# A transformer block on one core: four DRAM additions move to other places on GpSimd, and the planner no longer reserves time for them

## The chip, the cores and the metric

The kernel runs on 1 core of one Trainium2 chip. The metric is the device time of one execution in microseconds; lower is better. The engines are TensorE (PE in the profile; PEld is its loading of weights), VectorE (DVE), ScalarE (ACT), GpSimd (POOL) and SyncE (SP), which only issues DMAs here. GpSimd can issue DMAs too; its queue is the only one that can add to what stands at the destination.

## What is computed

One decoder block in float32 on 512 tokens of width 1024: a norm, a projection into queries, keys and values, attention of two kinds, an output projection, a gated MLP with a short convolution, and a gated embedding at the end. Cut to what matters:

```python
proj = rmsnorm(x, attn_pre_g) @ w_in
o_nsa = nsa_attention(q_n, k_cmp, v_cmp, ksl, vsl, kwn, vwn, gates, slopes)  # 8 heads, 2 groups
o_swa = swa_attention(q_s, k_s, v_s, sinks, slopes)                          # 8 heads, 2 groups, window 128
mix = concat([o_nsa, o_swa]) @ w_o
x = x + rmsnorm(mix, attn_post_g)
a, u = split(rmsnorm(x, mlp_pre_g) @ w_gate_up)                              # 2816 wide each
y = (gelu(causal_dwconv(a)) * u) @ w_down
x = x + rmsnorm(y, mlp_post_g)
x = x + (p @ w_ple) * sigmoid(x @ w_ple_gate)
```

## The kernel before

**Precision and work.** Each float32 operand is split into a high and a low part, and a product is made of three TensorE products (high by high, low by high, high by low). So each weight tile costs a load by SP, a conversion on ACT (the high part) and a subtraction on DVE or GpSimd (the low part). For part of the MLP, products of blocks are combined by sums of weights, which saves products on TensorE. Some of these sums, of blocks of the down projection, are made ahead of time in DRAM.

**The DRAM sums.** With `DRAM_SUMS = 1`, one scratch tensor `downblocks` in DRAM gets four blocks of 384 KB by plain copies from SP (`down_copies`, in the order of blocks 2, 3, 0, 1). Then four accumulating DMAs on GpSimd's queue (`down_additions`, through `accumulate`) add to them: block 2 gets an input block, block 3 gets an input block, block 0 gets block 3, block 1 gets block 0. So the third addition reads what the second made, and the fourth what the third made. The sums are read much later, by the down projection from 459 us on.

**The attention.** `attention` walks through 16 units: 8 of the first kind (`nsa_scores`) and 8 local ones (`swa_scores`), each for a group `g` of heads and a tile `qt` of 128 queries, in the order qt = 3, 0, 2, 1. Of a local unit, TensorE makes the scores (`swa_pss`), DVE takes row maxima, ACT the exponentials, DVE the reciprocal sums, GpSimd scales the four heads' rows (`scale_rows`, four TENSOR_SCALAR on `swa_u`), TensorE transposes them (`swa_pst`), ACT and DVE split them, and TensorE multiplies with the values (`swa_pso`). Between these products, TensorE is fed "fillers", among them the first part of the output projection: `out_proj_first` is called for output tiles 0 to 3 (four blocks of the mix each) and then for tiles 4 to 7 (six blocks each). Its inner function `w(c)` loads the weights of output tile `c`, with the low part on GpSimd (`fill_wh<-fill_wr` on POOL).

**What sets the order.** From the start of the kernel to the end of the output projection, the instructions are not issued at once but recorded as nodes (`Recorder`). `play` then plans an order: it gives each node a cost (`cost`, times `MARGIN` except on TensorE, plus `more`), simulates the five engines in six passes with due times from the pass before, keeps the best order and issues the nodes in it, each held in program order. A node's `then` is a list of further calls that are made right behind it; the planner does not see them. A node's `more` is extra planned time that stands for them.

**Where the additions are.** Each of the first calls of `w(c)` takes a copy and hangs it behind its weight load on SP. For c = 1, 2, 3 and 6 (`ADDS_AT`) it also hangs the next addition behind its subtraction on GpSimd and gives that node `more = ADD_US`, 1.35 us.

**Behind the attention.** `out_proj` records the rest of the output projection, loads of the embedding weights and tiles (`pletiles`), the sums of squares of the result (`outproj_s`), and the first MLP weights (`upw`); then it calls `rec.play`. `norm_add` follows: TensorE sums the squares over the partitions (`r_pst<-ones,outproj_s`), GpSimd takes the inverse root (`r2c`), and the first MLP products wait for the rows that are scaled by it.

Of the kernel before, what the change touches and what calls it, by code (L numbers as in the profile page):

```python
# [20 lines left out]
KC = D // P  # L21
# [59 lines left out]
MARGIN = 1.08  # L81
# [21 lines left out]
ETAGS = ["mm", "mm"]  # L103
D_AT = 1
T_DUE = (15, 20, 30, 34, 38, 42)
ADD_US = 1.35
ADDS_AT = (1, 2, 3, 6)
DRAM_SUMS = 1


# [73 lines left out]
class Node:  # L184
    ins = None

    def __init__(self, n, engine, name, a, k):
        self.n, self.engine, self.name, self.a, self.k = n, engine, name, a, k
        self.deps, self.after, self.wait = set(), [], 0
        self.then, self.more = [], 0.0  # L190
        views = [x for x in a if isinstance(x, View)]
        named = [(m, x) for m, x in k.items() if isinstance(x, View)]
        first = [k["out"]] if "out" in k else [x for x in a[:1] if isinstance(x, View)]
        self.writes = first + [x for m, x in named if m == "accum_out"]
        self.reads = [x for x in views if not any(x is w for w in self.writes)] + [x for m, x in named if m not in ("out", "accum_out")]
        self.tiles = list({id(x.tile): x.tile for x in self.writes + self.reads}.values())
        self.end = None
# [37 lines left out]
class Recorder:  # L235
# [71 lines left out]
    def link(self):  # L307

        for x in self.nodes:
            for d in x.deps:  # L310
                d.after.append(x)
        for x in self.nodes:
            x.cost = self.cost(x) * (1 if x.engine == "PE" else MARGIN) + x.more
            x.port = x.engine == "POOL" or x.engine == "DVE" and x.name in SHARED and not any(v.tile.psum for v in x.reads)
            x.key = x.n if x.engine != "SP" else min([y.n for y in x.after] or [x.n])

# [124 lines left out]
class Block:  # L441
# [564 lines left out]
    def swa_scores(self, u):  # L1006
        self.phase = "swa"
        nc = self.nc
        g, qt = u["g"], u["qt"]
        kh, kl = self.ks  # L1010
        n = P if qt == 0 else 2 * P
        k0 = 0 if qt == 0 else (qt - 1) * P
        b0 = P if qt == 0 else 0

        p = self.u([P, P_WIDTH], F32, "p")[:, : 4 * (2 * P + 1)].rearrange("p (r n) -> p r n", r=4)
        ns = self.nsink[:, 4 * g : 4 * g + 4]
        nc.gpsimd.tensor_copy(p[:, :, n], ns)
        nm = self.tiny([P, 4], "nm")
        for r in range(4):
            if r % 2 == 0:  # L1020
                ps = self.ps("s")
            o = ps[:, r % 2 * 256 : r % 2 * 256 + 256]
            self.score(ps, o, self.q[4 + 2 * g + r // 2][:, r % 2, qt * P : (qt + 1) * P],
                       kh[:, g, k0 : k0 + 256], kl[:, g, k0 : k0 + 256])
            nc.vector.tensor_tensor_reduce(p[:, r, :n], o[:, :n], self.dist_w[:, b0:], op0=ALU.add, op1=ALU.min,
                                           scale=SLOPES[4 * g + r], scalar=ns[:, r : r + 1], accum_out=nm[:, r : r + 1])
            yield 100 if r < 3 else 4 * n + 380
        sm = self.tiny([P, 4], "sm")
        for r in range(4):
            nc.scalar.activation(p[:, r, : n + 1], p[:, r, : n + 1], AF.Exp, bias=nm[:, r : r + 1], scale=-1.0,  # L1030
                                 accum_out=sm[:, r : r + 1])
        rc = self.tiny([P, 4], "rc")
        nc.vector.reciprocal(rc, sm)
        for r in range(4):
            self.scale_rows(p[:, r, :n], rc[:, r : r + 1])
        yield 400
        u["blocks"] = [
            ([p[:, r, b * P : (b + 1) * P] for r in range(4)], P,
             self.vs[k0 // P + b][:, 4 + g].rearrange("p a d -> p (a d)"))
            for b in range(n // P)  # L1040
        ]
# [105 lines left out]
    def attention(self):  # L1147
# [48 lines left out]
        units += [dict(kind="s", g=g, qt=qt) for g in range(2) for qt in (3, 0, 2, 1)]  # L1196
        self.x1 = [None] * 4
        self.raws = {}
        copies, adds = self.down_copies(), self.down_additions()
        self.down_work = ((next(copies, None), next(adds) if i in ADDS_AT else None) for i in range(KC))  # L1200

        def fetch(key, src, tag):
            t = self.u([P, D], F32, tag)
# [56 lines left out]
    def out_proj_first(self, cs, n):  # L1260

        def w(c):
            at = len(self.rec.nodes)
            r = self.weight(self.io["wo"][c][:, : n * P], n * P, lo="pool")
            copy, add = next(self.down_work, (None, None))
            for x in self.rec.nodes[at:]:
                if copy and x.engine == "SP":
                    x.then.append(copy)
                if add and x.engine == "POOL":
                    x.then.append(add)  # L1270
                    x.more = ADD_US
            return r

        wts = [w(cs[0])]
        for i, c in enumerate(cs):
            if i + 1 < len(cs):
                wts.append(w(cs[i + 1]))
            ps = self.ps("mm")
            yield from self.mixmm(ps, wts[i], range(n))
            self.nc.scalar.activation(self.mo[c // 2][:, c % 2, :], ps, AF.Copy)  # L1280

    def out_proj(self):
        self.phase = "outproj"
        nc, io = self.nc, self.io
        acc = self.s([P, T])
        NS = 3
        run = lambda gen: [None for _ in gen]
        first = []
        for c in range(KC):
            if c < NS:  # L1290
                if c == 0:

                    first = [(self.ps(t), self.weight(io["wo"][i][:, 4 * P :], 4 * P, tag=w))
                             for i, (t, w) in enumerate((("mm", "tt"), ("s", "wh"), ("mm", "wh")))]
                    self.pinned = self.steps[-1]
                    for ps, wt in first:
                        run(self.mixmm(ps, wt, range(4, 6), 0, False))
                    self.pinned = None
                ps, wt = first[c]
                run(self.mixmm(ps, wt, range(6, 8), 2, True))  # L1300
            else:
                if c < SIX:
                    k = 4
                    wt = self.weight(io["wo"][c][:, k * P :], (KC - k) * P)
                else:
                    k = 6
                    if c == SIX:

                        n = KC - SIX
                        last = self.weight(io["wo"][SIX:, :, k * P :].rearrange("c p n -> p c n"), n * 2 * P)  # L1310
                    wt = [w[:, (c - SIX) * 2 * P : (c - SIX + 1) * 2 * P] for w in last]
                ps = self.ps("smsms"[c - NS] .replace("m", "mm"))
                run(self.mixmm(ps, wt, range(k, KC)))
            m = self.mo[c // 2][:, c % 2, :]
            nc.vector.tensor_add(m, m, ps)
            self.square_acc(acc, m, c == 0, True)
            if c == 2:
                ple = self.ple_load()
                self.phase = "outproj"
            if c == 4:  # L1320
                for j in range(4):
                    if j < 2:
                        x1 = self.raws[f"x{j}"].rearrange("p (c n) -> p c n", c=2)
                    else:
                        x1 = self.u([P, 2, T], F32, "p")
                        self.load_late(x1, io["xT"][:, 2 * j : 2 * j + 2, :])
                    self.x1[j] = x1
            if c == KC - 1:
                self.upw = [self.weight(self.raws[f"gu{i}"], early=True, keep=True) for i in range(2)]
                self.upw += [self.weight(io["gu"][i], tag=("tt", "u")[i - 2], keep=True) for i in range(2, NB)]  # L1330
        live = [(t, 0.0) for t in (*ple[0], *ple[1][0])] + [(acc, 3.2), *((t, 2.5) for t in ple[1][1])]
        live += [(t, 4.0) for t in (*self.mo, *self.x1, *ple[2])] + [(t, 7.0) for w in self.upw for t in w]
        self.rec.play(live, BEGIN, self.hold)
        self.h2, self.f2 = [], []
        self.acc3 = self.norm_add(acc, "r2", C_GPOST, self.mo, self.x1, C_GMLP, self.h2, ple, 0)

# [802 lines left out]
    def run(self):  # L2139
        self.consts()  # L2140
        self.attention()
        self.tc.cur_priority = LATE
        self.out_proj()
        self.mlp_up()
        self.mlp_down()
        self.ple_gate()
# [62 lines left out]
```

## Time and profile before

| | |
|---|---|
| Time, median of 3 runs | 625.67 us (625.45 to 626.41) |
| Profiled execution | 626.01 us, span 624.3 us |
| PE busy | 618.3 us (99%), 4037 products |
| DVE busy | 510.6 us (82%) |
| ACT busy | 399.3 us (64%) |
| POOL busy | 156.1 us (25%), 239 instructions |
| DMA | 95.79 MB, mean 153 GB/s |
| GpSimd's DMA queue (q0) | 4880 packets, 10.49 MB |

The stages stand in the profile as follows: the load and first projections until about 70 us, the attention until about 212 us, the rest of the output projection and the norm until about 241 us, the MLP's first half until about 475 us, its second half until about 595 us, and the gated embedding to the end.

How to read it: a timeline row gives the start in us, the time that the merged instructions took, the engine, the line, the operation, "written tile <- read tiles", the shape, the count, and in brackets the idle time before it and who ended it. Lines L216 and L435 are the helpers that issue all instructions, so one goes by tiles. Matmuls overlap, and their durations are modelled; differences between starts are the safer measure on PE. The issue of a DMA on GpSimd stands as DMA_DIRECT2D on POOL.

### The profile page before, as it was taken

How to read it: one execution, taken by the hardware profiler on the slowest of the kernel's cores; microseconds unless marked ns; L12 is line 12 of the kernel's file. 1: busy time of each engine (PE TensorE's matmuls, PEld its weight loads, DVE VectorE, ACT ScalarE, POOL GpSimd, SP SyncE). 2: the span in 40 equal slices, each digit the busy share in tenths (PEclk: the TensorE clock that was granted, in tenths of full speed). 3: DMA queues.
4: the chain of work that ended last, by engine and by line, in shares of the span. 5: the costliest groups of instructions: out<-in, count | busy, mean ns of one | idle time of the engine just before them, and what ended most of it. 6: DMA issues, size and time to landing. Idle time of an engine off the chain costs nothing.

```text
span 624.3 us, 11286 instructions
## 1 busy us (share of the span) xinstructions
PE 618.3 (99%) x4037; PEld 560.3 (90%) x4037; DVE 510.6 (82%) x1038; ACT 399.3 (64%) x776; POOL 156.1 (25%) x239
## 2 busy tenths in 40 slices
PE   9999999999999999999999999999999999999997
PEld 8988888888888887888999999999998899999986
DVE  6697569978866498799999999999999876947973
ACT  7546579889899577565677767777753443434251
POOL 2011397787788100121010101101000001201000
PEclk9999999999999999999999999999999999999999
DMA  8427923404422658285467777786443433378032
GB/s 295 163 94 208 240 83 93 111 22 125 117 77 69 218 237 336 91 242 158 119 147 209 184 176 178 191 213 163 99 135 117 136 93 110 95 286 300 6 120 83
DMA packets 45576, 95.79 MB, mean 153 GB/s; under 512 B 4560, under 2 KB 14160, under 8 KB 45264
## 3 DMA queue, kind: packets, MB, share of 16 engines
q1 hardware_dynamic: 40496, 84.57, 41.2%
q0 software_dynamic: 4880, 10.49, 10.0%
q8 instruction: 32, 0.52, 0.4%
q14 instruction: 24, 0.20, 0.1%
q10 hardware_dynamic: 144, 0.00, 0.0%
HBM read 81.42 MB, written 9.44 MB: 146 GB/s over the span
## 4 chain that ended last, share of the span: by engine, by line
PE 98%; DVE 1%; ACT 0%; issue 0%; ACTq 0%
PE mlpup_psmm L216 23%; PE fill_psmm L435 10%; PE mlpup_pss L216 8%; PE mlpdown_pst L216 6%; PE mlpup_pst L216 5%; PE mlpdown_pss L216 4%; PE mlpdown_psmm L216 4%; PE nsa_pss L435 3%; PE nsa_pso L435 3%; PE nsa_pst L435 3%; PE norm_pss L216 3%; PE projq_psmm L435 3%; PE vnatural_pss L435 2%; PE mlpup_pso L216 2%; PE projk_psmm L435 2%; PE compress_psmm L435 2%
## 5 line engine op out<-in xcount | busy, mean ns | idle before, releaser
L216 PE MATMUL mlpup_psmm<-r_u,mlpup_wh 128*128 128x256 f32 (+1 forms) x612 | 75.2, 276 | 0.0
L216 PEld LDWEIGHTS mlpup_psmm<-r_u,mlpup_wh 128*128 128x128 f32 x612 | 72.2, 188 | 0.2
L216 PE MATMUL mlpup_psmm<-mlpup_u,mlpup_wh 128*128 128x256 f32 (+1 forms) x474 | 67.1, 292 | 0.0
L216 PEld LDWEIGHTS mlpup_psmm<-mlpup_u,mlpup_wh 128*128 128x128 f32 x474 | 61.1, 188 | 2.6
L216 POOL DMA_DIRECT2D mlpup_u<-in_gs_dram x17 | 20.7, 1220 | 147.8 <-DVE mlpup_s L216 54.8
L216 ACT ACTIVATE mlpup_wh<-mlpup_u 128x1024 fp32r<-128x1024 f32 (+1 forms) x38 | 39.4, 1038 | 14.4 <-PE mlpup_psmm L216 10.8
L216 ACT ACTIVATE mlpdown_wh<-mlpdown_wr 128x1024 fp32r<-128x1024 f32 (+1 forms) x24 | 23.5, 981 | 34.6 <-DMA mlpdown_wr<-in_down_dram 9.2
L216 DVE TENSOR_TENSOR mlpup_wh<-mlpup_u,mlpup_wh 128x1024 fp32r<-128x1024 f32 (+1 forms) x38 | 45.1, 1190 | 0.3 <-ACT mlpup_wh L216 0.3
L435 PE MATMUL fill_psmm<-loadx_u,fill_wh 128*128 128x512 f32 x144 | 44.9, 400 | 0.0
L216 PE MATMUL mlpdown_pst<-mlpup_u,mlpdown_wh 128*128 128x512 f32 (+1 forms) x228 | 44.5, 337 | 0.0
L216 PEld LDWEIGHTS mlpdown_pst<-mlpup_u,mlpdown_wh 128*128 128x128 f32 x228 | 36.6, 188 | 4.8
L435 POOL TENSOR_SCALAR nsa_u<-nsa_u,nsa_nrc,vnatural_u 128x512 f32<-128x512 f32 (+3 forms) x64 | 38.4, 614 | 8.1 <-DVE nsa_nrc L435 6.6
L216 POOL TENSOR_TENSOR mlpdown_s<-mlpdown_s,mlpdown_s 128x512 f32<-128x512 f32 x6 | 10.1, 1692 | 120.5 <-ACT mlpdown_s L216 120.4
L216 DVE TENSOR_TENSOR mlpdown_wh<-mlpdown_wr,mlpdown_wh 128x1024 fp32r<-128x1024 f32 (+1 forms) x24 | 26.9, 1122 | 15.5 <-ACT mlpdown_wh L216 11.8
L435 ACT ACTIVATE nsa_u<-nsa_u,nsa_nnm 128x512 f32<-128x512 f32 (+3 forms) x64 | 35.4, 556 | 2.0 <-DVE nsa_nnm L435 1.7
L216 PE MATMUL mlpdown_pss<-mlpup_u,mlpdown_wh 128*128 128x256 f32 x246 | 34.9, 276 | 0.0
L216 DVE TENSOR_TENSOR mlpup_wh<-mlpup_wr,mlpup_wh 128x1024 fp32r<-128x1024 f32 (+1 forms) x23 | 27.9, 1211 | 5.9 <-ACT mlpup_wh L216 5.9
L216 PEld LDWEIGHTS mlpdown_pss<-mlpup_u,mlpdown_wh 128*128 128x128 f32 x246 | 31.5, 188 | 0.5
L216 ACT ACTIVATE mlpup_u<-mlpup_u 128x512 fp32r<-128x512 f32 (+1 forms) x36 | 21.5, 624 | 16.3 <-DVE mlpup_u L216 16.2
L216 PE MATMUL mlpdown_psmm<-mlpup_u,mlpdown_wh 128*128 128x256 f32 (+1 forms) x180 | 31.1, 317 | 0.0
L435 DVE CUSTOM_DVE_ANT_0 nsa_u<-nsa_pss,vnatural_u 128x128 f32<-128x128 f32 (+4 forms) x64 | 27.3, 445 | 3.3 <-PE nsa_pss L435 1.7
L435 POOL TENSOR_TENSOR fill_wh<-fill_wr,fill_wh 128x1024 fp32r<-128x1024 f32 (+2 forms) x13 | 24.9, 1918 | 17.5 <-DMA compress_u<-projk_u 9.3
(346 smaller groups left out, 1655.4 us busy)
## 6 DMA issues: line engine op xcount, KB each, us to landing
mlpup_u<-in_gs_dram SPq DMA_DIRECT2D x34, 512.0 KB, 5.5
mlpup_u<-in_gs_dram POOLq DMA_DIRECT2D x17, 512.0 KB, 6.0
mlpup_wr<-in_gs_dram SPq DMA_DIRECT2D x17, 256.0 KB, 2.8
fill_wr<-in_win_dram SPq DMA_DIRECT2D x6, 512.0 KB, 4.1
fill_u<-fill_u SPq DMA_DIRECT2D x20, 128.0 KB, 2.3
mlpdown_wr<-in_down_dram SPq DMA_DIRECT2D x5, 512.0 KB, 4.7
compress_u<-projk_u SPq DMA_DIRECT2D x16, 128.0 KB, 3.5
kept_e<-pletiles_u SPq DMA_DIRECT2D x4, 512.0 KB, 5.2
```

What stands on the lines that cost most here:

```text
L216: return f(*map(real, a), **{m: real(x) for m, x in k.items()})
L435: hold(x.call(*map(real, x.a), **{m: real(v) for m, v in x.k.items()}))
```

## The change

The planner's extra cost is removed: the constants `ADD_US` and `ADDS_AT`, the field `more`, and its part in the node's cost. The four additions hang in new places: the first still behind the subtraction of output tile 1's weights; the second and third behind the last scaling of rows of the local units (g = 0, qt = 0) and (g = 1, qt = 0); the fourth is issued right behind `rec.play`, so behind everything that was recorded. The copies stay behind the weight loads of output tiles 0 to 3. Nothing else differs.

```diff
             for d in x.deps:
                 d.after.append(x)
         for x in self.nodes:
-            x.cost = self.cost(x) * (1 if x.engine == "PE" else MARGIN) + x.more
+            x.cost = self.cost(x) * (1 if x.engine == "PE" else MARGIN)
...
         nc.vector.reciprocal(rc, sm)
         for r in range(4):
             self.scale_rows(p[:, r, :n], rc[:, r : r + 1])
+        if qt == 0:
+            self.rec.nodes[-1].then.append(self.adds[1 + g])
         yield 400
...
-        copies, adds = self.down_copies(), self.down_additions()
-        self.down_work = ((next(copies, None), next(adds) if i in ADDS_AT else None) for i in range(KC))
+        self.copies, self.adds = list(self.down_copies()), list(self.down_additions())
...
             r = self.weight(self.io["wo"][c][:, : n * P], n * P, lo="pool")
-            copy, add = next(self.down_work, (None, None))
             for x in self.rec.nodes[at:]:
-                if copy and x.engine == "SP":
-                    x.then.append(copy)
-                if add and x.engine == "POOL":
-                    x.then.append(add)
-                    x.more = ADD_US
+                if x.engine == "SP":
+                    x.then += self.copies[c : c + 1]
+                elif x.engine == "POOL" and c == 1:
+                    x.then.append(self.adds[0])
             return r
...
         self.rec.play(live, BEGIN, self.hold)
+        self.adds[3]()
         self.h2, self.f2 = [], []
```

More of the change, by code (lines that the diff above doesn't have):

```diff
@@ L105 @@
 T_DUE = (15, 20, 30, 34, 38, 42)
-ADD_US = 1.35
-ADDS_AT = (1, 2, 3, 6)
 DRAM_SUMS = 1
@@ L189, in __init__ @@
         self.deps, self.after, self.wait = set(), [], 0
-        self.then, self.more = [], 0.0
+        self.then = []
         views = [x for x in a if isinstance(x, View)]
```

## The prediction

> **What bounds the kernel now.** I read the page first, then the waits of PE, then PE's timeline in the one stretch where it loses time, then GpSimd's timeline (POOL) around the four additions, and last the stretch behind the attention where one of them is put.
>
> ```profile
> span 624.3 us, 11286 instructions
> PE 618.3 (99%) x4037; PEld 560.3 (90%) x4037; DVE 510.6 (82%) x1038; ACT 399.3 (64%) x776; POOL 156.1 (25%) x239
> ...
> PE 98%; DVE 1%; ACT 0%; issue 0%; ACTq 0%
> ```
> ```profile
> PE swa_pso L435 <- DVE swa_u L435: 0.2, 1, 0.2
> ```
>
> The chain that ended last is PE for 98% of the span, and behind the start PE waits visibly once, for 0.2 us. GpSimd is busy a quarter of the span. So nothing that is taken off GpSimd shows in the time unless PE was waiting for it, and anything that makes PE wait shows in full. A busy PE can hide lost time in a stretched matmul, so I compare starts with starts.
>
> ```profile
> 163.26 1.19 PE L435 MATMUL swa_pss<-projq_u,fill_u 128*128 128x256 f32 x8
> 164.29 0.63 PE L435 MATMUL fill_psmm<-projq_u,fill_wh 128*128 128x512 f32 x2
> 164.76 0.60 PE L435 MATMUL swa_pst<-ident,nsa_u 128*128 128x128 f32 x4
> 165.11 0.71 PE L435 MATMUL fill_psmm<-projq_u,fill_wh 128*128 128x512 f32 x2
> ...
> 169.33 0.27 PE L435 MATMUL swa_pst<-ident,swa_u 128*128 128x128 f32 x1
> 169.72 0.47 PE L435 MATMUL swa_pso<-compressout_u,vc 128*128 128x512 f32 x1
> 170.03 0.71 PE L435 MATMUL swa_pst<-ident,swa_u 128*128 128x128 f32 x5
> 170.50 2.08 PE L435 MATMUL swa_pss<-projq_u,fill_u 128*128 128x256 f32 x12
> 172.69 0.47 PE L435 MATMUL swa_pso<-swa_u,vnatural_u 128*128 128x512 f32 x1
> 173.32 0.73 PE L435 MATMUL swa_pso<-swa_u,vnatural_u 128*128 128x512 f32 x2 [0.16 <-DVE swa_u L435]
> ```
>
> The first four rows give the pace: 8 score products in 1.03 us, 0.13 each; 2 wide ones in 0.47, 0.235 each; 4 transpositions in 0.35, 0.09 each. Against it the transposition at 169.33 holds PE for 0.39 (0.30 lost), the 12 products at 170.50 for 2.19 instead of 1.55 (0.64 lost), the product at 172.69 for 0.63 (0.39 lost). Together 1.33 us are lost between 169.3 and 173.3, in the first local units. That is nearly all that a better order of the attention could win.
>
> ```profile
> 160.00:180.00 20.00, 19.47 (x112) 16.01 (x111) 17.09 (x59) 18.57 (x55) 15.45 (x29) 1.00 0.35 81
> ```
>
> The columns are the stretch, its length, then PE, PE's weight loads, DVE, ACT, POOL, the granted clock (1.00, so no throttle) and the DMA share. ACT is busy 18.57 of 20 us there and DVE 17.09, POOL 15.45: the stall hangs on ACT and DVE first.
>
> **The change part by part.** The span is 624.3, the profiled execution took 626.01, so 1.71 us lie around the span; the median of the three runs, 625.67, is 0.34 below that execution. I sum changes and put them on the median. About 0.2%, 1.25 us, is what a measurement of this kernel can tell from no change: faster means below 624.4, slower above 626.9.
>
> ```profile
> 149.50 1.01 POOL L216 DMA_DIRECT2D downblocks<-in_gd_dram  x1
> 150.35 1.51 POOL L435 TENSOR_SCALAR nsa_u<-nsa_u,nsa_nrc,vnatural_u 128x384 f32<-128x384 f32 x2
> 163.39 0.81 POOL L216 DMA_DIRECT2D downblocks<-in_gd_dram  x1
> 164.00 0.42 POOL L435 COPY swa_u<-nsink 128x4 f32<-128x4 f32 x1
> 165.41 1.30 POOL L435 TENSOR_TENSOR fill_u<-fill_s,fill_u 128x512 fp32r<-128x512 f32 x1 [0.99 <-ACT fill_u L435]
> 171.09 1.41 POOL L435 TENSOR_SCALAR swa_u<-swa_u,swa_rc 128x128 f32<-128x128 f32 x4 [1.61 <-DVE swa_rc L435]
> 173.69 0.74 POOL L435 TENSOR_TENSOR nsa_u<-swa_s,nsa_u 128x256 fp32r<-128x256 f32 x1 [1.19 <-ACT nsa_u L435]
> 189.69 1.42 POOL L435 TENSOR_SCALAR swa_u<-swa_u,swa_rc 128x128 f32<-128x128 f32 x4 [0.40 <-PE fill_psmm L435]
> 191.07 1.85 POOL L435 TENSOR_TENSOR fill_wh<-fill_wr,fill_wh 128x768 fp32r<-128x768 f32 x1
> 210.22 0.73 POOL L435 TENSOR_TENSOR swa_u<-swa_s,swa_u 128x256 fp32r<-128x256 f32 x1 [3.86 <-ACT swa_u L435]
> 236.60 1.04 POOL L216 TENSOR_TENSOR r2c<-r_rv,mhalf 128x4 f32<-128x4 f32 x1 [25.64 <-DVE r_rv L216]
> ```
>
> An addition keeps GpSimd from its next instruction for 0.85 us (149.50 to 150.35) or 0.61 (163.39 to 164.00). Going through the places:
>
> - Addition 0 stays behind the weights of output tile 1, at 149.5. It loses its 1.35 us in the plan. Actual issue as before: 0 us. If the new order leaves no room there, the scaling queued behind it and the transpositions on PE that read it are late by up to 0.85. Bounds 0 and +0.85; I take 0, since the instruction stands there now and PE loses nothing around it.
> - Addition 1 leaves 163.39 and goes behind the last scaling of local unit (0, 0), which ended near 172.5; GpSimd then waited 1.19 us for ACT, until 173.69. The issue of 0.6 fits: 0 us. Without that pause, the split queued behind it is late by 0.6. Taking it from 163.39 gains nothing on PE either: 0.99 us of idle time followed there, more than the 0.61.
> - Addition 2 goes behind the last scaling of unit (1, 0). There GpSimd has no pause: 189.69 + 1.42 meets the output weights at 191.07. Those weights start 0.6 us later, but they were followed by an addition of their own until now, which leaves. 0 us, bounds 0 and +0.6.
> - Addition 3 goes behind everything recorded. GpSimd ends at 210.95 and has nothing until 236.60, so the issue of 0.6 us and its wait for addition 2 delay no GpSimd work. It does compete for the DMA engines, the next part.
>
> **The transfer at the end of the attention.** This is the part that speaks against the change.
>
> ```profile
> q0 software_dynamic: 4880, 10.49, 10.0%
> ...
> downblocks<-downblocks POOLq DMA_DIRECT2D x2, 384.0 KB, 5.2
> ```
> ```profile
> 212.00:227.00 15.00, 15.00 (x67) 12.34 (x66) 10.22 (x14) 8.69 (x13) 0.00 (x0) 1.00 1.02 391
> 218.00:233.00 15.00, 15.00 (x67) 12.35 (x66) 14.08 (x21) 10.85 (x16) 0.00 (x0) 1.00 0.64 258
> ```
> ```profile
> 217.32 1.15 ACT L435 ACTIVATE pletiles_u<-swa_u 128x512 fp32r<-128x512 f32 x2 [1.48 <-DMA swa_u<-in_pT_dram]
> 218.56 1.06 ACT L435 ACTIVATE pletiles_wh<-swa_u 128x1024 fp32r<-128x1024 f32 x1
> 219.57 1.06 ACT L435 ACTIVATE outproj_wh<-outproj_wr 128x1024 fp32r<-128x1024 f32 x1
> ```
> ```profile
> 217.98 0.69 DVE L435 TENSOR_TENSOR pletiles_u<-swa_u,pletiles_u 128x512 fp32r<-128x512 f32 x1 [0.89 <-ACT pletiles_u L435]
> 230.77 2.27 DVE L435 TENSOR_TENSOR outproj_s<-outproj_s,outproj_s 128x512 f32<-128x512 f32 x3
> ```
> ```profile
> 233.25 0.95 PE L216 MATMUL r_pst<-ones,outproj_s 128*128 128x1 f32 x8
> ```
>
> Landing takes an addition about 5.2 us, and each stands at least 15 us behind the one whose sum it reads, so GpSimd waits for none. GpSimd's queue q0 took 10.0% of the 16 engines' 624.3 us, 62.4 us, for 10.49 MB. An addition moves 384 KB, 0.393 MB: 62.4 x 0.393 / 10.49 = 2.3 us of all engines (an estimate from that row). Issued at 211, it comes at the head of 15 us in which the DMA engines are full (share 1.02). The loads behind it slip by up to 2.3 us. ACT waits for one of them (1.48 us, to 217.32); DVE follows ACT (0.89 us, to 217.98) and then works 14.08 of 15 us until 233, when it has the sum of squares that PE reads at 233.25. So DVE can make up 15 - 14.08 = 0.92 us, and its last addition ends at 230.77 + 2.27 = 233.04, 0.2 ahead of PE. A slip s thus costs PE about s - 1.1 us. Before, the same 2.3 us lay in stretches like 160 to 180, where the DMA share was 0.35, and cost nothing. Lower bound 0 (a slip of 1.1 or less); s = 2.3 gives +1.2; if the loads lost the whole landing time of 5.2, +4.1. No gain is possible, since nothing leaves this stretch. I take s = 1.8, close to the estimate but less than it, because part of the addition's packets fall before 212 to 213, when the engines are not yet full: +0.7.
>
> The Trainium skill, "DMA: Bandwidth & Descriptors", section "Queues, rings and completion order", says that each DMA engine takes the queues that have work in turn, packet by packet. By that rule the loads of SP would pay the whole 2.3 us before the late one lands, and the sum would be +1.2 here in place of +0.7.
>
> **The order of the attention.** Dropping the 1.35 us four times from the planner's costs changes the written-out order on all engines before 230 us. The trace of before can't show the new order. Its bounds are, below, the 1.33 us lost at 169.3 to 173.3, and above, the 0.85 and 0.6 us of issues that no plan holds room for, +1.45. The old plan held 1.35 where 0.6 to 0.85 was used, so GpSimd's splits and the conversions on ACT ahead of them were hurried for nothing, in a stretch where ACT is the tightest; that points to a gain. But the stall's last releaser is DVE, not POOL. I take half of the stall, -0.6.
>
> Sum: 0 + 0 + 0 + 0.7 - 0.6 = +0.1, so 625.67 + 0.1 = 625.8 us; on the profiled execution 626.1, span 624.4.
>
> **The rivals.**
>
> - *Forecast, no measurable change* (625.8; its own range 624.5 to 626.9). For it: the chain is PE, and its only recoverable loss is 1.33 us, hardly over the bound. Chance 0.57.
> - *The new order clears the stall and the late transfer hides.* -1.33 + 0 gives 624.3. For it: addition 1 gets a real pause and ACT's hurried conversions are relaxed. Against: the stall hangs on ACT and DVE, busy 18.57 and 17.09 of 20. Chance 0.17.
> - *The last addition holds up the loads behind the attention*, and PE pays at the sum of squares. It decides over a slip of 1.1 us; alone it makes the kernel measurably slower from a slip of 2.35. At 2.3 with the old stall kept, 626.9; at 5.2, 629.8; between them, at s = 3.1, +2.0 and 627.7. For it: DMA share 1.02 there, DVE busy 14.08 of 15. Against: 2.3 us of engine time is the estimate. By the skill's rule of turns (named above) the slip is the whole 2.3, which puts the kernel at this edge. Chance 0.20.
> - *The pauses are not there*: in the new order addition 0 and addition 2 push scalings and weights on PE's path, so the change doesn't issue in pauses at all. +1.45 gives 627.1. For it: the row at 191.07 follows without a gap. Against: both places hold an addition within 2 us already. Chance 0.06.
>
> **How the numbers follow.** Likeliest 625.8. The range 624.1 to 627.9 holds the forecast, the faster rival's 624.3, the slower rivals' 627.7 and 627.1, and leaves out the upper half of the loads' rival (to 629.8) and gains past the stall. Faster by over 0.2%: 0.17. Within: 0.57. Slower: 0.20 + 0.06 = 0.26.
>
> **What would show it.** In the profile after, four GpSimd DMAs: near 149, near 172 in a gap, near 191, near 211; if the last is elsewhere, the term of +0.7 is void. The load that ACT waits for until 217.32 should arrive 1 to 2 us later against the end of the attention, and DVE's last sum of squares should meet PE's product at 233 with no margin; if PE starts that product without delay, the loads' part is wrong. Starts between 169 and 174 should show 0.3 to 1 us lost; none lost, or a stall at another place over 1 us, would make the forecast wrong, as would any PE wait behind 245 us, where nothing is changed.

## The result and the profile after

The changed kernel takes 631.73 us (median of 22 runs, 624.96 to 634.30) against 625.93 (22 runs, 625.35 to 626.41): the ratio is 1.0075, 95% interval 1.0049 to 1.0102. It is slower, and outside the predicted range of 624.1 to 627.9.

The median hides the shape. The 22 runs fall into two groups with nothing between them: 7 short ones from 624.96 to 627.03 and 15 long ones from 630.83 to 634.30. The kernel before has no long run. Two runs at a lower granted clock, 1038.49 us (0.56) of one kernel below and 770.34 us (0.75) of the kernel before, are left out of all ratios and counts. So there are two questions: what the change did to a short run, which is what the prediction argued about, and where the long runs come from.

The profiled execution was a short run, 625.32 us. Its page and its waits of PE:

```profile
span 623.6 us, 11282 instructions
PE 617.5 (99%) x4037; PEld 558.9 (90%) x4037; DVE 511.3 (82%) x1038; ACT 398.8 (64%) x776; POOL 156.8 (25%) x239
...
PE 91%; DMA 3%; DVE 3%; POOL 1%; issue 1%; ACT 1%; SPq 0%; DVEq 0%; POOLq 0%
```
```profile
PE outproj_psmm L433 <- DVE outproj_wh L433: 0.3, 1, 0.3
PE r_pst L214 <- DVE outproj_s L433: 0.2, 1, 0.2
```

The span is 0.7 us shorter than before. The chain of work that ended last now leaves PE from 185.7 to 232.5 us and runs through DVE, POOL, ACT and loads, and the single wait of PE in the attention has given way to two behind it. The timeline of GpSimd shows the four additions:

```profile
148.93 1.02 POOL L214 DMA_DIRECT2D downblocks<-in_gd_dram  x1
...
168.96 1.41 POOL L433 TENSOR_SCALAR swa_u<-swa_u,swa_rc 128x128 f32<-128x128 f32 x4 [1.78 <-DVE swa_rc L433]
170.31 0.81 POOL L214 DMA_DIRECT2D downblocks<-in_gd_dram  x1
172.01 0.73 POOL L433 TENSOR_TENSOR nsa_u<-swa_s,nsa_u 128x256 fp32r<-128x256 f32 x1 [0.89 <-ACT nsa_u L433]
...
189.25 0.70 POOL L214 DMA_DIRECT2D downblocks<-downblocks  x1
...
209.19 0.83 POOL L214 DMA_DIRECT2D downblocks<-downblocks  x1
235.93 1.04 POOL L214 TENSOR_TENSOR r2c<-r_rv,mhalf 128x4 f32<-128x4 f32 x1 [25.91 <-DVE r_rv L214]
```

They stand where the change says, and the second has a real pause behind it (0.89 us left). The stall of the attention is mostly gone: from the starts of PE's products, each step against the median step of its shape, 160 to 180 us lost 1.84 us before and loses 0.60 now. The window shows it as a full PE with 116 products where there were 112:

```profile
160.00:180.00 20.00, 20.00 (x116) 16.78 (x115) 16.29 (x56) 18.91 (x54) 14.77 (x29) 1.00 0.41 99
```

The load that ACT waits for behind the attention is later, as the prediction said: issued at 209.29 us, it lands 8.1 us behind its issue, where it took 6.3 us before (the row of before, at 217.32, stands in the prediction). In the trace of only the last addition moved, an experiment below, it takes 8.1 us too.

```profile
217.42 1.15 ACT L433 ACTIVATE pletiles_u<-swa_u 128x512 fp32r<-128x512 f32 x2 [3.04 <-DMA swa_u<-in_pT_dram]
```

PE's timeline behind the attention shows the price of the fourth addition's transfer:

```profile
222.90 1.20 PE L433 MATMUL outproj_psmm<-swa_u,outproj_wh 128*128 128x512 f32 x4 [0.32 <-DVE outproj_wh L433]
...
232.51 0.69 PE L214 MATMUL r_pst<-ones,outproj_s 128*128 128x1 f32 x5 [0.19 <-DVE outproj_s L433]
```

The brackets give 0.32 and 0.19 us of idle time; by starts, 220 to 240 us loses 0.96 us where it lost nothing (-0.09) before. So far the short run is what was forecast in kind, with both terms larger: -1.24 for -0.6 and +1.05 for +0.7.

**The long runs.** A second profiled execution of the same kernel, in the first experiment below, was a long one. Three fences with the same windows (behind the length stand PE's busy time and its count of products; the clock is third from the end): before, after in its short run, after in its long run.

```profile
300.00:320.00 20.00, 20.00 (x179) 20.00 (x178) 18.13 (x25) 15.13 (x26) 1.21 (x1) 1.00 0.54 148
320.00:440.00 120.00, 120.00 (x1062) 120.00 (x1061) 114.75 (x152) 88.03 (x151) 14.61 (x12) 1.00 0.71 184
```
```profile
320.00:440.00 120.00, 120.00 (x1061) 120.00 (x1060) 114.67 (x152) 88.17 (x152) 14.61 (x12) 1.00 0.71 181
```
```profile
span 632.3 us, 11282 instructions
...
300.00:320.00 20.00, 20.00 (x173) 20.00 (x173) 17.85 (x25) 15.09 (x26) 1.20 (x1) 1.00 0.54 149
320.00:440.00 120.00, 120.00 (x1021) 120.00 (x1020) 111.56 (x146) 84.93 (x146) 14.61 (x12) 1.00 0.68 175
```

PE is busy all the time in all three, the clock is 1.00, and no wait of PE is listed in this stretch. Yet in the long run PE gets through 1021 products in 120 us where it otherwise does 1061. Between starts, a 128x256 product takes 117.78 ns instead of 113.33. These 40 products are worth 40 x 113.33 ns = 4.5 us. Of the 8.7 us by which the spans differ, another 0.6 lie between 300 and 320, 3.1 behind 440 and 0.4 in the first 20 us. The pace changes at one point, at 305.1 us here, and at the same product, between 303.5 and 305.3, in each of the four long runs with a profile. That is over 90 us behind the last thing that the change moved.

The place is the start of the group of products in the second blocked tile of the MLP that first uses the low weights `mlpup_wh`, made by DVE. First the kernel before, then the long run, PE and DVE in each:

```profile
303.88 1.52 PE L216 MATMUL mlpup_psmm<-mlpup_u,mlpup_wh 128*128 128x256 f32 x12
305.24 0.96 PE L216 MATMUL mlpup_psmm<-r_u,mlpup_wh 128*128 128x256 f32 x7
```
```profile
303.88 1.22 DVE L216 TENSOR_TENSOR mlpup_wh<-mlpup_u,mlpup_wh 128x1024 fp32r<-128x1024 f32 x1
```
```profile
305.03 1.16 PE L214 MATMUL mlpup_psmm<-r_u,mlpup_wh 128*128 128x256 f32 x8
```
```profile
303.81 1.22 DVE L214 TENSOR_TENSOR mlpup_wh<-mlpup_u,mlpup_wh 128x1024 fp32r<-128x1024 f32 x1
```

Before, DVE ends at 305.10 and PE's group starts at 305.24, 0.14 later. In the long run DVE ends at 305.03, at the very start of the group. Its eight products should take 7 x 0.113 + 0.276 = 1.07 us (seven steps and the 0.276 us that the profile gives one product) and take 1.16: PE hitched. One step between starts is 172 ns, and from there on every step is 117 to 119. In the short run of the same kernel the hitch is there too (a step of 163 ns), and PE went back to 113. So the lateness of these weights is a property of the changed kernel; what PE does after the hitch varies. The trace shows what PE waits for: in all five profiles with the hitch, the load of these low weights into PE starts 52 to 54 ns behind DVE's end, and 43 to 59 ns behind the start of the product ahead of it. In the eight others it starts 3 to 5 ns behind that product. The short run's 56 ns lies among those of the long runs.

DVE is busy 19.7 of the 20 us from 280 to 300, so it carries a lateness along. Measured against PE, DVE's starts agree in both kernels to 0.03 us until 270.2 us (in the time of before), and after has them 0.11 us later from 270.8 and 0.14 us later from 274.4 up to these weights. What lies ahead of 270.8 is one instruction of ACT, an activation of the MLP. ACT's timeline, before, then the short run after:

```profile
269.80 1.53 ACT L216 ACTIVATE mlpup_u<-mlpup_s,cols 128x512 f32<-128x512 f32 x2 [1.06 <-DVE mlpup_s L216]
```
```profile
269.40 1.52 ACT L214 ACTIVATE mlpup_u<-mlpup_s,cols 128x512 f32<-128x512 f32 x2 [1.30 <-DVE mlpup_s L214]
```

Same wait for the same DVE result, 0.24 us more of idle time. Before, it starts 60 ns behind the instruction in which ACT waits for DVE; after, 340 ns. ACT does nothing in between that the trace shows. The trace also shows two DMAs of 8 KB that load instructions; they come at 262.5 and 263.0 us before, at 268.8 and 271.8 after. That suggests that ACT was late because of where it stood in its own code. So does a count of ACT's records in the trace, waits included: this activation is the 577th before and the 576th after.

### The profile page after: what moved, and what is told of

It reads as the page before. It is cut to its first block, busy times and chain, and to the rows that moved or that the text cites. A ratio compares the mean times of both kernels' runs of the same rounds, so it can differ in the third digit from the quotient of the medians.

```text
span 623.6 us, 11282 instructions
## 1 busy us (share of the span) xinstructions
PE 617.5 (99%) x4037; PEld 558.9 (90%) x4037; DVE 511.3 (82%) x1038; ACT 398.8 (64%) x776; POOL 156.8 (25%) x239
## 4 chain that ended last, share of the span: by engine, by line
PE 91%; DMA 3%; DVE 3%; POOL 1%; issue 1%; ACT 1%; SPq 0%; DVEq 0%; POOLq 0%
PE mlpup_psmm L214 23%; PE mlpup_pss L214 8%; PE fill_psmm L433 7%; PE mlpdown_pst L214 6%; PE mlpup_pst L214 5%; PE mlpdown_pss L214 4%; PE mlpdown_psmm L214 4%; PE nsa_pss L433 3%; PE nsa_pso L433 3%; PE nsa_pst L433 3%; PE norm_pss L214 3%; PE projq_psmm L433 3%; PE mlpup_pso L214 2%; PE vnatural_pss L433 2%; PE projk_psmm L433 2%; PE compress_psmm L433 2%
```

## The experiments

There were eleven runs. The first four look for the part of the change that makes long runs.

**The change again**, without an edit.

> The kernel after, unchanged, for a second profile. Its 22 runs so far lie in two groups, 8 from 625.0 to 627.0 us and 14 from 630.8 to 634.3, and the one profile is of the first group. Theory A (the last addition slips the loads behind the attention, by very different amounts): both groups again, and if the profile is of the long group, ACT's wait for the loads between 212 and 230 us is longer by 5 to 9 us and PE stands there that long. Theory B (the new order of the attention is what sometimes stalls): the same two groups, but the lost time lies before 210 us.

633.87 us (4 runs, 633.37 to 634.01), ratio 1.0131 (1.0117 to 1.0145). All four are long; the long profile above is one of them. (The 22 runs that the expectation counts divide into 7 and 15, not 8 and 14.)

**The last addition back** behind output tile 6, still without time for it in the plan. On GpSimd, the issue of this one DMA, with the waits around it, is all that changes its place.

```diff
-                elif x.engine == "POOL" and c == 1:
-                    x.then.append(self.adds[0])
+                elif x.engine == "POOL" and c in (1, 6):
+                    x.then.append(self.adds[0 if c == 1 else 3])
...
-        self.adds[3]()
```

> The kernel after, with the last addition back behind the subtraction of output tile 6's weights on GpSimd (no planned time for it). Theory A: one group, 624 to 625.5 us in all runs, since the loads behind the attention have the DMA engines to themselves and the attention keeps its gain. Theory B: two groups as in the kernel after, median above 630.

633.01 us (4 runs, 632.34 to 633.12), ratio 1.0119 (1.0103 to 1.0134).

**Only the last addition moved**, in the kernel before, with its plan kept.

```diff
-                    x.then.append(add)
+                    if c == 6:
+                        self.last_add = add
+                    else:
+                        x.then.append(add)
...
+        self.last_add()
```

> The kernel before, with only the last addition moved behind the recorded part; its 1.35 us stay in the plan, so that the planned order is that of before. Theory A: two groups, 626 to 628 and 631 to 636, most runs in the upper one. Theory B: one group near 625.9, at most 1.2 above.

626.61 us (11 runs, 625.85 to 627.43), ratio 1.0017 (1.0008 to 1.0026): no long run, and 0.9 us slower. Its timeline has the wait that the fourth addition brings, and by starts 0.84 us are lost between 220 and 240 us:

```profile
223.96 1.20 PE L435 MATMUL outproj_psmm<-swa_u,outproj_wh 128*128 128x512 f32 x4 [0.29 <-DVE outproj_wh L435]
```

**The last addition later still**, behind the norm's start.

```diff
-        self.adds[3]()
         self.h2, self.f2 = [], []
         self.acc3 = self.norm_add(acc, "r2", C_GPOST, self.mo, self.x1, C_GMLP, self.h2, ple, 0)
+        self.adds[3]()
```

> The kernel after, with the last addition issued behind the second norm's instructions on GpSimd (after 257 us) instead of at the end of the attention. Theory A: one group, 624 to 625.5, the same as with the addition back in the attention. Theory B: two groups, median above 630. A third case, that an accumulation between two blocks of the scratch tensor is slow wherever other transfers run: still some runs above 630.

632.90 us (4 runs, 632.66 to 633.04), ratio 1.0116 (1.0102 to 1.0130); 0.02 us are lost between 220 and 240.

So the place of the last addition, theory A, has nothing to do with the long runs: they stay with the addition moved either way, and do not come with the addition alone. That also speaks against the third case, a slow addition between blocks wherever other transfers run. The addition costs 0.9 us where it was put. Theory B, the new order, holds in so far as the long runs come with it; but none of the lost time lies before 210 us, as B had it.

The next four test the chain that the traces suggest, called theory C: late activation on ACT at 270 us, DVE late, low weights late at 304, hitch of PE, slower pace. Its rival D says that the new order of the attention sets the pace itself and the rest is company. Two experiments act at the head of the chain, two in the middle.

**Padding.** The changed kernel with ACT's tiny warming activation at the start issued six times, which moves every later ACT instruction on in its code (the activation is now the 581st record) and leaves the order as it is.

```diff
-        nc.scalar.activation(first, self.ones, AF.Copy)
+        for _ in range(6):
+            nc.scalar.activation(first, self.ones, AF.Copy)
```

> The changed kernel with the tiny warming activation at the start of ScalarE's program issued six times in place of once: five more instructions of a few tens of ns while ScalarE has nothing to do, so that every later instruction lies five places on in its code; the order of work is the same. Theory C (an 8 KB load of ScalarE's instructions that in the changed kernel falls at 268.8 us, as a pause of ScalarE ends, delays one activation by 0.3 us; VectorE stays 0.13 us late; the low weights of the second blocked tile arrive 0.05 us late at 304 us; TensorE's narrow products then mostly keep 117.8 ns in place of 113.3 ns to 573 us): the load falls inside the pause again, the idle time ahead of that activation goes from 1.30 back to 1.06 us, no run above 628, median 624.5 to 626. Rival D (the new order of the attention, or a state carried from it, sets TensorE's pace, and the late weights are only its company): median 631 to 634 in most runs.

625.41 us (11 runs, 624.65 to 626.07), ratio 0.9995 (0.9987 to 1.0004). Not one long run. ACT's timeline:

```profile
268.60 1.53 ACT L214 ACTIVATE mlpup_u<-mlpup_s,cols 128x512 f32<-128x512 f32 x2 [1.03 <-DVE mlpup_s L214]
```

The lateness is gone (1.03 instead of 1.30), with five instructions of no use at the other end of the kernel.

**The reverse in the kernel before.** Its one warming activation is left out, so ACT's code moves one place the other way, and the activation is the 576th record as in the changed kernel. The order of before is kept.

```diff
-        first = self.tiny([P, 1], "act", bufs=1)
-        nc.scalar.activation(first, self.ones, AF.Copy)
```

> The kernel before without its one tiny warming activation at the start of ScalarE's program: each later ScalarE instruction lies one place (or two, with a wait of its own) earlier in its code, and the order of work is that of before; its activation table is loaded ahead of the first scaling of x, which may cost up to 1.3 us at the start. Theory C: the 8 KB loads of ScalarE's instructions move past the pause at 262 to 269 us, towards 268.8 us as in the changed kernel; if they do, the idle time ahead of the activation at 269.8 us goes from 1.06 to about 1.30 us and most runs lie 6 to 9 us above before, at 632 to 635; if the load still falls inside the pause, 625 to 627. Rival D: 625 to 627 wherever the load falls.

634.11 us (5 runs, 632.03 to 636.17), ratio 1.0141 (1.0122 to 1.0160). All five are long, without any part of the change. ACT, PE, DVE and the window in its profile:

```profile
269.98 1.52 ACT L216 ACTIVATE mlpup_u<-mlpup_s,cols 128x512 f32<-128x512 f32 x2 [1.33 <-DVE mlpup_s L216]
```
```profile
305.14 1.03 PE L216 MATMUL mlpup_psmm<-r_u,mlpup_wh 128*128 128x256 f32 x7
```
```profile
303.92 1.22 DVE L216 TENSOR_TENSOR mlpup_wh<-mlpup_u,mlpup_wh 128x1024 fp32r<-128x1024 f32 x1
```
```profile
320.00:440.00 120.00, 120.00 (x1021) 120.00 (x1020) 111.56 (x146) 84.86 (x146) 14.61 (x12) 1.00 0.68 177
```

Each link is there: idle 1.33 instead of 1.06, DVE's end at 305.14 exactly at PE's start, seven products in 1.03 us instead of 0.96, and 1021 products in the window.

**Halves of the low weights.** The changed kernel with the low weights of the second blocked tile made in two halves; the first product waits for the half it reads.

```diff
-        self.split_ops((j, "A"), xs, D, t - 3 * step, (((j, "x"), "load"),), ready=t - 10, frees=(xtag,), low_deps=((j, "x1"),))
+        self.split_ops((j, "A"), xs, D, t - 3 * step, (((j, "x"), "load"),), ready=t - 10, frees=(xtag,), low_deps=((j, "x1"),), halves=n == 1)
...
-            ("1", product("q", "A", 0, x(0, a), wide=n == 0), (lo("A"),) + begin, copy("p", "q"), -1),
-            ("2", product("p", "A", 4, x(1, a), ends=True), ((j, "copy", "1"),), None, 0),
+            ("1", product("q", "A", 0, x(0, a), wide=n == 0), (((j, "A"), "lo0") if n == 1 else lo("A"),) + begin, copy("p", "q"), -1),
+            ("2", product("p", "A", 4, x(1, a), ends=True), ((j, "copy", "1"), lo("A")), None, 0),
```

> The changed kernel with the low weights of the second blocked tile's first product made in two halves of 512 columns, the first product waiting for the first half alone: the weights are there about 0.5 us ahead of TensorE in place of 0.05 us behind it; the code load of ScalarE stays at 268.8 us. Theory C: no hitch of TensorE at 304 us, products of 113.3 ns from there on, median 625 to 626, no run above 628. Rival D: median 631 to 634 in most runs, pace of 117.8 ns from about 304 us.

625.60 us (12 runs): nine from 625.09 to 625.96, three from 633.35 to 633.90. Its profiled, short run has ACT's lateness (idle 1.31 us) and no hitch; seven products take 0.96 us:

```profile
305.25 0.96 PE L214 MATMUL mlpup_psmm<-r_u,mlpup_wh 128*128 128x256 f32 x7
```

**The same halves with the last addition back**, the edit that puts the addition back and the one above together.

> The changed kernel with the last addition back in its old place (behind the POOL subtraction of the seventh output tile) and the same halves in the second blocked tile. Theory C: as the version with the halves alone, and without the two short waits of TensorE at 222 and 232 us that came with the later addition (0.8 to 1.0 us): median 623.5 to 625, shorter than both kernels. Rival D: median 631 to 633.

Of eleven runs, nine lie between 624.30 and 624.93, two at 632.73 and 632.92; without the halves all four were long.

Both cures work, as theory C has it, and the one at the head works fully: 0 of 11 long runs with padding. The halves bring the long runs from 19 of 26 (after and its repetition) to 3 of 12, and from 4 of 4 to 2 of 11. That is most of it, but "no run above 628" was wrong. Rival D fails on all four. These four were measured on one chip, so that a difference between chips does not explain them.

The last three close gaps.

**Halves in the kernel with the warming activation left out.** It tells whether the late weights or the place of ACT's code itself (rival E) sets the pace.

> The kernel before without its tiny warming activation (whose five runs all took 632 to 636 us) and with the halves of the second blocked tile made in the helpful order. Theory C: the late activation at 270 us stays (idle 1.33 us), the first product finds its weights, and most runs come back to 625 to 627. Rival E: 632 to 636 in most runs, since the code load lies where it lay.

627.53 us (10 runs): four from 625.39 to 625.75, five from 627.43 to 628.26, one at 633.42, where without the halves all were long. ACT's activation is as late as there:

```profile
271.92 1.52 ACT L216 ACTIVATE mlpup_u<-mlpup_s,cols 128x512 f32<-128x512 f32 x2 [1.33 <-DVE mlpup_s L216]
```
```profile
320.00:440.00 120.00, 120.00 (x1061) 120.00 (x1060) 115.05 (x152) 88.30 (x151) 14.62 (x12) 1.00 0.71 187
```

With ACT late and the weights on time, PE keeps 1061 products in the window. Only four of the ten runs lie in the expected 625 to 627, but nine lie clear of the 632 to 636 of rival E, which falls. The profiled run, 628.26, loses 1.7 us more than before within its first 20 us, and not in the MLP. PE waits 0.7 us for ACT there, whose table load now comes later; but the run without the halves has this wait too and loses no more than before in that stretch, so what made the difference stays open.

**The halves turned round, in the kernel before**, so that the half that is needed first comes last.

```diff
...
             a, b = slice(0, n // 2), slice(n // 2, n)
+            if turned:
+                a, b = b, a
...
```

> The kernel before with the low weights of the second blocked tile's first product made in two halves, the half that TensorE needs first made last; order and ScalarE's code up to 300 us are those of before. By the two halves in the version with halves (1.29 us together in place of 1.22) the needed weights come 0.07 us later, 0.07 us ahead of the first product in place of 0.14. Theory C with a threshold at the hitch: no hitch or one of under 0.03 us, and 625 to 627; if the weights come later than that and the hitch shows, 632 to 635. Rival E (not the late weights but the place of ScalarE's code load itself sets the pace): 625 to 627 even with a hitch of 0.05 us or more.

625.76 us (10 runs, 625.04 to 626.09), ratio 0.9998 (0.9989 to 1.0007).

```profile
303.83 1.28 DVE L216 TENSOR_TENSOR mlpup_wh<-mlpup_u,mlpup_wh 128x512 fp32r<-128x512 f32 x2
```
```profile
305.19 1.07 PE L216 MATMUL mlpup_psmm<-r_u,mlpup_wh 128*128 128x256 f32 x8
```

DVE ends at 305.11, 0.08 ahead of PE, and eight products take the 1.07 us of no hitch. It fits C, but without a hitch it tells C from E in nothing. It does show how small the margin is: 0.08 us ahead is enough, 0.00 is not. That fits the 52 to 54 ns that lie between DVE's end and a load that waits for it.

**Padding with the last addition back**, the version that the findings point to.

> The changed kernel with the last addition back in its old place and ScalarE's tiny warming activation issued six times. Theory C: ScalarE's own 8 KB code load falls at about 256 us as in the version with the padding alone, no run above 628; without the two short waits of TensorE at 222 and 232 us that the later addition brought (0.8 to 1.0 us): median 624.3 to 624.9, shorter than both kernels in every run group. Rival D': the median stays at 625 to 626, the waits of 222 and 232 us having been hidden in the end of the kernel.

624.66 us (11 runs, 623.74 to 625.22), ratio 0.9980 (0.9971 to 0.9989): shorter than both kernels, and no long run. Its timeline has neither of the two waits behind the attention:

```profile
222.38 1.53 PE L433 MATMUL outproj_psmm<-swa_u,outproj_wh 128*128 128x512 f32 x6
...
231.96 0.98 PE L214 MATMUL r_pst<-ones,outproj_s 128*128 128x1 f32 x8
```

The loads of instructions, the place of the activation among ACT's records and its lateness; the last column counts the long runs:

| kernel | 8 KB instruction loads start at | place | idle ahead of the activation | long |
|---|---|---|---|---|
| before | 262.5, 263.0 | 577 | 1.06 | 0 of 22 |
| only the last addition moved | 262.8, 263.3 | 577 | 1.06 | 0 of 11 |
| before, halves turned | 262.4, 262.9 | 577 | 1.05 | 0 of 10 |
| after, padded | 256.3, 268.0 | 581 | 1.03 | 0 of 11 |
| last addition back, padded | 256.2, 268.0 | 581 | 1.03 | 0 of 11 |
| after | 268.8, 271.8 | 576 | 1.30 | 15 of 22 |
| after again | 269.8, 273.2 | 576 | 1.32 | 4 of 4 |
| last addition back | 267.6, 270.7 | 576 | 1.31 | 4 of 4 |
| last addition later | 267.4, 272.0 | 576 | 1.31 | 4 of 4 |
| before, warming left out | 262.4, 272.6 | 576 | 1.33 | 5 of 5 |
| after, halves | 269.0, 272.4 | 576 | 1.31 | 3 of 12 |
| last addition back, halves | 267.7, 271.5 | 576 | 1.32 | 2 of 11 |
| before, warming left out, halves | 264.3, 274.6 | 576 | 1.33 | 1 of 10 |

The activation is late in every profile where it stands at place 576, and in no other.

## Why the prediction was wrong

- **The failed step** is the reach given to the new order: it "changes the written-out order on all engines before 230 us", its upper bound was +1.45, and behind 245 us there stood "where nothing is changed". The work there is unchanged, but not the place of each ACT instruction in its code. One ACT record fewer ahead of it made one activation start 340 instead of 60 ns behind its wait, and a margin of 0.14 us, 35 us further on, was gone. From there on the long runs lose 8 us. The prediction named a PE wait behind 245 us as a sign that it was wrong; the loss is there, but it does not even show as a wait. That this order hit that place is bad luck; that an order can reach behind its own stretch is what the prediction left out.
- **The stall of the attention** was put at half of 1.33 us, -0.6. The order clears nearly all of it: -1.24 by starts; the kernel with the last addition back and padding is 1.2 us below before. The mechanism was right and the size too small.
- **The fourth addition's transfer** was put at +0.7, with a slip of the loads that ends at the sum of squares. Both waits stand there, at 222.9 on the late weights and at 232.5 on the sum. The slip was sized well: the load lands 1.8 us later behind its issue (8.1 against 6.3), as s = 1.8 had it. The time measured +0.9 for the addition alone (626.61 against 625.72) and +0.75 between the two padded kernels (625.41 against 624.66). It is not paid in each run: the padded kernel's profiled run, one of its shortest at 624.84, loses only 0.04 us in that stretch. By the rule of turns in the Trainium skill, "DMA: Bandwidth & Descriptors", section "Queues, rings and completion order", the estimate was +1.2, from a slip of 2.3 us; the trace's 1.8 us and the runs lie below that.
- **The first three additions** were put at 0, and no wait on them shows. The issue of the third (0.64 us at 189.3) does lie on the chain that ended last; but it stands at the same place in the padded kernel with the last addition back, whose profile loses no more between 180 and 240 us than that of the kernel before, to 0.1 us.
- **The sum.** With the padding, the change as made takes 625.41 us, against the 625.8 of the forecast: -1.2 + 0.8 = -0.4. Without the mishap it would have been no measurable change, the verdict that was forecast. That the sum comes so near is in part luck, since a gain taken at half its size and a cost taken somewhat too small offset each other.

Shown by cure and by provocation: ACT's place in its code makes the activation late, and the late weights make the long runs. Not settled are three things. The first is how a load of instructions delays ACT. The trace does not say which engine a load serves; of the two, padding ACT moves the one at 271.8 to 256.3, and leaving an activation out moves the one at 263.0 to 272.6, while the other stays within 1 us. So the load that goes with the lateness starts 2.4 to 3.3 us after the late activation, not at 268.8 as the expectation on record had it. The second is why a hitch of 40 to 60 ns leaves PE at another pace, in some runs and not in others. The third is what makes the 6 of 33 long runs that stay with the halves; no profile shows one. The short profiled run of the halves with the last addition back has a small hitch at another load, one that waits for ACT (a step of 130 ns at 302.73 us, the pace stays at 113), so other thin margins may play a part; that is not shown.

## What to carry to other kernels

When an order is planned anew, compare the two profiles behind the place of the change too, by counting products in equal windows: a PE that is busy throughout, without waits and at full clock, can still be 4% slower. Look for margins of a tenth of a microsecond between a saturated engine and the one that bounds the kernel, and widen them, because an instruction added or removed elsewhere can use them up. When one kernel's runs form two groups, take a profile of each before any theory is made; and to tell a change from its side effect on the place of code, measure it once more with a few idle instructions at the start.

## What the runs showed of the hardware

- Back-to-back 128x256 float32 products have two paces, 113.33 and 117.78 ns, at a granted clock of 1.00. A step of 153 to 172 ns, where the weights came at the last moment, is followed by the slower one in the four long runs with a profile, and it holds for more than 250 us; in a short run a step of 163 ns is followed by the faster one. In the kernel before, too, products behind four one-column products at 568.6 us go on at 117 to 118 ns. Products of 512 columns take 229 ns in short and long runs alike.
- A weight load that waits for VectorE starts 52 to 54 ns behind the end of the VectorE instruction, in the five profiles in which it comes too late.
- One ScalarE activation starts 340 to 354 ns behind its wait where it is the 576th of the engine's records, and 60 to 63 ns behind it where it is the 577th or 581st. Five idle activations of ScalarE at the start of the kernel took the long runs away (631.73 us, with 15 of 22 long, to 625.41 us with none), and leaving one out of the kernel before brought them: 634.11 us instead of 625.80.
